# Projecting v, k and q of the first half of the tokens 512 columns at a time instead of 256

## The chip, the cores and the metric

The kernel runs on one core of one Trainium2 chip. The metric is the device time of one execution in microseconds (us); lower is better. The kernel before was timed in three runs: 2037.11, 2034.74 and 2035.24 us, median 2035.24 us. One further execution was profiled.

## The reference, cut to what matters

One layer of a streaming encoder is computed for 2048 prompt tokens and for 64 sample tokens of a running stream. All values are 32-bit floats.

```
h = rmsnorm(x, norm_g) @ w_in          # (tokens, 1024) @ (1024, 6144)
qa, ka, va, za, qb, kb, vb, zb, ga, gb = split(h)
qa, ka = rmsnorm per head of 64        # differential attention: q, k
k_prompt, v_prompt = ka, va            # outputs (also k_sample, v_sample)
oa = diff_attention(qa, ka, va)        # 4 heads, block-causal, ALiBi
ob = retention(qb, kb, vb)             # 4 heads, chunk by chunk
y  = x + (ga * (oa' @ w_oa) + gb * (ob' @ w_ob)) @ w_out
```

The change concerns the columns qa, ka and va (512 columns each) of the product with `w_in`, for prompt tokens 0 to 1023 and the 64 sample tokens.

## The kernel before, in words

**Products in three parts.** Every 32-bit operand of a large product is split into a high and a low part (`wh`, `wl` of the weights, `xh`, `xl` of the tokens) of a type that TensorE multiplies in one pass. A product is then three matmuls: high by high, high by low, low by high (`mm_group`, L375 to L390; the matmul is L384).

**Two halves.** The tokens are handled in two halves of 1024; the 64 sample tokens go with the first. For each half the normed tokens lie transposed in on-chip memory (`xh`, `xl`), and the 6144 columns of `w_in` are streamed past them. One pass over all tokens of a half with one block of columns is called a sweep here. There are 24 sweeps of 256 columns per half.

**Natural and transposed sweeps.** v, k, q and vb are computed by `natural` (L392): the tokens are the stationary operand (a tile of 128 tokens, or 64 for the sample tile), 256 columns of W are the moving one, and two token tiles share one PSUM bank (`mm`, two banks). The first half has nine token tiles, so a sweep has 9 x 24 matmuls. All other columns go through `transposed` (L548), where W is stationary and up to 512 tokens move.

**The supply of W.** A sweep needs four W units of 256 x 256. `w_load` (L332) brings each with one DMA of 256 KB into a staging buffer (`ws`, three of them). `w_split` (L344) casts it on ScalarE (`wh`, L354) and subtracts on GpSimd (`wl`, L361; the first and third on VectorE, L358); that frees the staging buffer. Units lie in the tag `w`: 12 buffers, a high and a low one to a unit, so six units. `mm_group` gives a unit back in the last token tile of the sweep (L388).

**Evacuation.** A finished bank is taken over by `fin_va` (L496: high part, plain copy, low part, three DMA stores) or `fin_qk` (L417: squares, gain, norm per head, transposes on TensorE at L466, high and low part of the transposed result, stores to `kT` or `qT` and for k to the output).

**The order of work.** The program plans itself: tasks are Python generators with priorities, `loop` (L80) emits the instructions of the most urgent task that is ready by the planner's own clock of the engines, and the order so found is fixed on TensorE, ScalarE and VectorE (L1546, L1564). The DMA queue on SyncE and the order on GpSimd are left to the framework. The projections (`w_stream`, L1442) have the lowest priority, attention (`z_stream`, L1497) goes ahead of them. Attention of half h starts when the mark `kqv0h` is set; heads 2 and 3 wait for `kqv1h` (L690). `ORD` (L1572) lists the sweeps of the two halves with these marks: in the first half v0, v1, k0, k1, q0, mark, q1, mark; in the second v0, k0, q0, mark, v1, k1, q1, mark. After that come vb, qb, kb, a mark for retention, and the gates. When all projections are stored, `out_stream` does the output projections.

**The start.** `x_prep` and `x_norm` (L247, L272) load and norm the token tiles, at most five in flight; `x_tile` (L298) transposes them on TensorE. The first sweep is told by `fresh` to wait for each token tile as it becomes ready.

**Buffers of the attention.** The pool `att` holds `K` (4 buffers), `V` (4) and `q` (2), each of 4 KB per partition; before the first attention they are empty. `load_head` (L649) and `load_q` (L674) fill them from the stores of the projections.

Of the kernel before, what the change touches and what calls it, by code (L numbers as in the profile page):

```python
# [54 lines left out]
class Hybrid:  # L55
# [105 lines left out]
    def consts(self):  # L161
# [11 lines left out]
        self.qinv = c("qinv", [128, 2, 8])  # L173
        for h in range(4):
            for u in range(2):
                nc.vector.memset(self.qinv[:, h // 2, 4 * u + 2 * (h % 2):4 * u + 2 * (h % 2) + 2],
                                 (SLOPES[h] / 0.125) ** 2 / 64.0)
        self.gq = c("gq", [128, 1])
# [153 lines left out]
    def w_load(self):  # L332
        for half in range(2):
            for c0 in self.order[half]:
                for q in range(4):
                    yield from self.take("ws")
                    st = self.sb(self.wp, [128, 2, 256], "ws")
                    t = self.ld(st, self.i["w_in"][0, 256 * q:256 * q + 256, c0:c0 + 256]
                                .rearrange("(c p) n -> p c n", p=128), 1 << 18)
                    self.wst.append((st, t))  # L340
                    self.wloads += 1
                    yield self.pe

    def w_split(self):  # L344
        nc = self.nc
        for n in range(4 * (len(self.order[0]) + len(self.order[1]))):
            yield lambda: len(self.wst) > 0
            st, t = self.wst.pop(0)
            yield from self.take("w", 2)
            if t > self.pe:  # L350
                yield t
            h = self.sb(self.wp, [128, 2, 256], "w", "wh", F32R)
            l = self.sb(self.wp, [128, 2, 256], "w", "wl", F32R)
            nc.scalar.copy(h, st)  # L354
            t = self.A(512, self.pe)
            if n in (0, 2):
                yield t
                nc.vector.tensor_sub(l, st, h.bitcast(F32))  # L358
                t = self.V(512, t)
            else:  # L360
                nc.gpsimd.tensor_sub(l, st, h.bitcast(F32))  # L361
                t = self.G(512, t)
            self.give("ws", t)
            self.wq.append((h, l, t))
# [10 lines left out]
    def mm_group(self, ps, n, us, wsl, x, wfirst, last):  # L375
        nc = self.nc
        seg, xsl = x
        for c in range(KC):
            a, b = yield from self.w_unit(us, c)
            a, b = a[:, wsl], b[:, wsl]  # L380
            xh, xl = self.xh[seg][:, c, xsl], self.xl[seg][:, c, xsl]
            ops = ((a, xh), (a, xl), (b, xh)) if wfirst else ((xh, a), (xh, b), (xl, a))
            for i, (p, q) in enumerate(ops):
                nc.tensor.matmul(ps, p, q, start=c == 0 and i == 0, stop=c == KC - 1 and i == 2)  # L384
                self.P(n)
            if c % 2:
                if last:
                    self.give("w", self.pe + LAT, 2)  # L388
                if c < KC - 1:
                    yield self.pe  # L390

    def natural(self, half, fin, fresh=False):  # L392
        us = []
        tiles = self.xtiles(half)
        for j0 in range(0, len(tiles), 2):
            pair = tiles[j0:j0 + 2]
            yield from self.take("mm")
            ps = self.psum("mm")
            for u, (src, r, seg, col) in enumerate(pair):
# [5 lines left out]
                if u < len(pair) - 1:  # L405
                    yield self.pe
            t0 = 1024 * half + 128 * j0 if j0 < 8 else T
            self.spawn(fin(ps[:r, :256 * len(pair)], r, len(pair), t0, self.pe + LAT), 0, "w")
            yield self.pe
# [7 lines left out]
    def fin_qk(self, which, g):  # L417
        nc = self.nc
        ep = self.ep

        def fin(ps, r, nu, t0, t):
            n, ng, rt = 256 * nu, 4 * nu, r * nu
# [21 lines left out]
            if which == "q":  # L444
                nc.vector.scalar_tensor_tensor(out=ms, in0=ms, scalar=64.0 * EPS,
                                               in1=self.qinv[:r, g, :ng], op0=ALU.add, op1=ALU.mult)
            else:
                nc.vector.tensor_scalar(ms, ms, 1.0 / 64, EPS, op0=ALU.mult, op1=ALU.add)
# [7 lines left out]
            if which == "k":  # L456
                if t0 < T:
                    dst = self.o["k_prompt"][0, 0, t0:t0 + rt, 2 * g:2 * g + 2]
                else:
                    dst = self.o["k_sample"][0, 0, :, 2 * g:2 * g + 2]  # L460
                ts = self.rows_out(dst.rearrange("t h c d -> t (h c d)"), raw, nu, 1 << 17)
            yield from self.take("tp")
            tp = self.psum("tp")
            for u in range(nu):
                for h in range(2):
                    nc.tensor.transpose(tp[:, h * rt + u * r:h * rt + u * r + r],  # L466
                                        raw[:, u * 256 + h * 128:u * 256 + h * 128 + 128],
# [5 lines left out]
            hi = self.sb(ep, [128, 512], "thi", dt=F32R)[:, :2 * rt]  # L473
            lo = self.sb(ep, [128, 512], "tlo", dt=F32R)[:, :2 * rt]
            pt = tp[:, :2 * rt]
# [12 lines left out]
            for d, s, tag, w in zip(dst, (hi, lo), ("thi", "tlo"), (t1, t2)):  # L488
                if w > self.pe:
                    yield w  # L490
                self.give(tag, self.st(d[2 * g:2 * g + 2, :, t0:t0 + rt].rearrange("h p t -> p h t"),
                                       s.bitcast(F32).rearrange("p (h t) -> p h t", h=2), nu << 17))
# [3 lines left out]
    def fin_va(self, g):  # L496
        nc = self.nc
        ep = self.ep

        def fin(ps, r, nu, t0, t):  # L500
            n, rt = 256 * nu, r * nu
# [13 lines left out]
            if t0 < T:  # L515
                dst = self.o["v_prompt"][0, 0, t0:t0 + rt, 2 * g:2 * g + 2]
            else:
                dst = self.o["v_sample"][0, 0, :, 2 * g:2 * g + 2]
            yield t1
            gsl = slice(256 * g, 256 * g + 256)  # L520
            self.give("thi", self.rows_out(self.vN[0][t0:t0 + rt, gsl], hi.bitcast(F32), nu, 1 << 17))
            yield t2
            td = self.rows_out(dst.rearrange("t h e -> t (h e)"), raw, nu, 1 << 17)
# [4 lines left out]
            self.give("tlo", self.rows_out(self.vN[1][t0:t0 + rt, gsl], lo.bitcast(F32), nu, 1 << 17))  # L528
# [913 lines left out]
    def w_stream(self):  # L1442
# [9 lines left out]
        first = ORD(fva0, fva, fk, fq, m0, m1)  # L1452
# [14 lines left out]
        self.order = [[c for c, _ in q if c is not None] for q in seqs]  # L1467
# [8 lines left out]
        for half in range(2):  # L1476
            for k, (c0, f) in enumerate(seqs[half]):
# [152 lines left out]
```

## Time and profile before

| what | before |
|---|---|
| timed runs, median | 2035.24 us |
| the profiled execution's own time | 2037.63 us |
| its span, first to last instruction | 2035.9 us |
| TensorE busy | 1999.1 us, 98% |
| TensorE weight loads busy | 1826.1 us, 90% |
| VectorE / ScalarE / GpSimd busy | 48% / 47% / 21% |
| DMA engines busy | 46.8% |
| granted TensorE clock, mean | 0.996 |

The span is a profiled execution's stretch from its first to its last instruction. The engines are PE (TensorE matmul), PEld (its weight loads, which overlap), DVE (VectorE), ACT (ScalarE), POOL (GpSimd) and SP (SyncE, which issues the DMAs). In a view by groups a row names the line, the engine, the operation, out<-in with shapes (partitions x elements; stationary operand first for a matmul), the count, the busy time and the mean of one in ns. In a timeline a row has the start in us, the duration in us and, in brackets, the idle time of the engine before it and what ended it. The duration of a matmul holds its whole way through the array, so that neighbours overlap: what a matmul costs in a stream is the distance from start to start. The view by windows gives, for each stretch, the busy time and the count of each engine, then the granted clock of TensorE, the share of DMA time and the bytes per second.

### The profile page before, as it was taken

The page shows a single profiled execution, that of the slowest core. Times are in us where ns is not written, and L with a number is a line of the kernel's source. Part 1 is how long each engine was busy: PE and PEld are TensorE (multiplying, and loading weights), DVE is VectorE, ACT ScalarE, POOL GpSimd, SP SyncE. Part 2 cuts the span into 40 slices and gives each one's busy share as a digit, 9 for nine tenths or more (in the row PEclk, how much of TensorE's full clock was granted, in tenths as well). Part 3 has the DMA queues.
Part 4 walks back from the last instruction along what each step waited for, and adds up shares of the span by engine and source line. Part 5 has one row for each costly group of instructions (what it writes and reads, how often), then busy time and mean ns, then how long its engine had stood idle before and what let it go on. Part 6 is the DMA issues. An engine that isn't in the chain of part 4 may idle for free. (4 is left out here: it accounts for less than half of the span.)

```text
span 2035.9 us, 35819 instructions
## 1 busy us (share of the span) xinstructions
PE 1999.1 (98%) x13058; PEld 1826.1 (90%) x13058; DVE 985.9 (48%) x2671; ACT 962.7 (47%) x2123; POOL 420.5 (21%) x394
## 2 busy tenths in 40 slices
PE   7999999999999999999999999999999979999999
PEld 7999999999998999999999888888888868888997
DVE  6265765643331210546856545635653365444442
ACT  5334766644343332535766655634654453333321
POOL 1222112121012221221211212122131343222210
PEclk9999999999999999999999999999999989999999
DMA  6663545345565463563352252463233665454531
GB/s 217 202 195 115 162 138 145 101 124 156 151 170 133 130 194 93 152 200 127 113 155 91 84 154 75 115 188 99 63 100 113 187 200 154 144 150 136 148 101 58
DMA packets 332160, 281.57 MB, mean 138 GB/s; under 512 B 65104, under 2 KB 307408, under 8 KB 331984
## 3 DMA queue, kind: packets, MB, share of 16 engines
q1 hardware_dynamic: 331984, 279.29, 46.8%
q8 instruction: 103, 1.69, 0.4%
q14 instruction: 73, 0.60, 0.1%
HBM read 187.71 MB, written 91.49 MB: 137 GB/s over the span
## 5 line engine op out<-in xcount | busy, mean ns | idle before, releaser
L384 PE MATMUL mm<-xh,wh 128*128 128x512 f32 (+2 forms) x1280 | 459.8, 359 | 0.0
L384 PE MATMUL mm<-xh,wl 128*128 128x512 f32 (+2 forms) x1280 | 452.0, 353 | 0.0
L384 PE MATMUL mm<-xl,wh 128*128 128x512 f32 (+2 forms) x1280 | 451.7, 353 | 0.0
L361 POOL TENSOR_TENSOR wl<-ws,wh 128x512 fp32r<-128x512 f32 x190 | 252.1, 1342 | 832.5 <-ACT wh L354 643.5
L384 PE MATMUL mm<-wh,xh 128*128 128x256 f32 x1088 | 313.3, 288 | 0.5 <-ACT xh L315 0.3
L384 PE MATMUL mm<-wl,xh 128*128 128x256 f32 x1088 | 307.7, 283 | 0.7 <-DVE wl L358 0.3
L384 PE MATMUL mm<-wh,xl 128*128 128x256 f32 x1088 | 307.7, 283 | 0.2 <-DVE xl L316 0.2
L384 PEld LDWEIGHTS mm<-xh,wl 128*128 128x128 f32 x1280 | 241.0, 188 | 31.1
L384 PEld LDWEIGHTS mm<-xh,wh 128*128 128x128 f32 x1280 | 241.3, 189 | 30.6 <-issue 0.2
L384 PEld LDWEIGHTS mm<-xl,wh 128*128 128x128 f32 x1280 | 241.4, 189 | 30.0
L384 PEld LDWEIGHTS mm<-wh,xh 128*128 128x128 f32 x1088 | 204.8, 188 | 3.3 <-ACT xh L315 0.5
L384 PEld LDWEIGHTS mm<-wl,xh 128*128 128x128 f32 x1088 | 204.9, 188 | 3.0 <-DVE wl L358 0.5
L384 PEld LDWEIGHTS mm<-wh,xl 128*128 128x128 f32 x1088 | 204.7, 188 | 0.4 <-DVE xl L316 0.4
L569 ACT COPY ev<-mm 128x512 f32<-128x512 f32 x140 | 71.6, 512 | 213.4 <-PE mm L384 200.4
L865 DVE TENSOR_TENSOR atl<-at,ath 128x512 fp32r<-128x512 f32 (+1 forms) x144 | 93.6, 660 | 151.6 <-ACT ath L863 151.6
L782 ACT ACTIVATE row<-row,a_mx 128x1024 f32<-128x1024 f32 (+7 forms) x160 | 153.5, 963 | 24.2 <-DVE a_mx L762 24.0
L752 DVE CUSTOM_DVE_ANT_0 row<-s,dfar 128x512 f32<-128x512 f32 (+2 forms) x192 | 117.3, 631 | 72.4 <-PE s L744 71.3
L354 ACT CAST wh<-ws 128x512 fp32r<-128x512 f32 x192 | 117.0, 619 | 65.4 <-PE mm L384 37.5
L863 ACT CAST ath<-at 128x512 fp32r<-128x512 f32 (+1 forms) x144 | 79.6, 563 | 99.1 <-PE at L850 98.6
L743 PE MATMUL s<-K,q 128*128 128x512 f32 (+3 forms) x320 | 120.3, 381 | 3.0 <-DVE a_acc L752 2.8
L803 DVE SCALAR_TENSOR_TENSOR row<-row,a_w 128x1024 f32<-128x1024 f32 (+4 forms) x96 | 101.4, 1064 | 40.5 <-ACT row L800 40.2
L744 PE MATMUL s<-K,q 128*128 128x512 f32 (+3 forms) x320 | 115.7, 363 | 0.0
(196 smaller groups left out, 3922.1 us busy)
## 6 DMA issues: line engine op xcount, KB each, us to landing
ws<-in_w_in_dram SPq DMA_DIRECT2D x192, 256.0 KB, 3.0
q<-qT SPq DMA_DIRECT2D x128, 128.0 KB, 3.0
V<-vN SPq DMA_DIRECT2D x24, 512.0 KB, 5.4
K<-kT SPq DMA_DIRECT2D x48, 256.0 KB, 4.2
gt<-gaT SPq DMA_DIRECT2D x64, 132.0 KB, 2.1
gt<-gbT SPq DMA_DIRECT2D x64, 132.0 KB, 2.1
xt<-in_x_prompt_dram SPq DMA_DIRECT2D x16, 512.0 KB, 5.0
kn<-in_cache_k_T_dram SPq DMA_DIRECT2D x32, 256.0 KB, 3.2
```

Source lines behind the costliest of these rows:

```text
L354: nc.scalar.copy(h, st)
L361: nc.gpsimd.tensor_sub(l, st, h.bitcast(F32))
L384: nc.tensor.matmul(ps, p, q, start=c == 0 and i == 0, stop=c == KC - 1 and i == 2)
L569: nc.scalar.copy(ev, ps)
L743: nc.tensor.matmul(ps, q1s, kk, start=True, stop=False)
L744: nc.tensor.matmul(ps, q2s, kk, start=False, stop=True)
L752: nc.vector.tensor_tensor_reduce(out=units[k0 // 1024][:, k0 % 1024:k0 % 1024 + n], in0=ps, in1=tab, scale=-SLOPES[h], scalar=3.0e38, op0= ...
L782: nc.scalar.activation(u, u, AF.Exp, bias=mx, scale=-1.0, accum_out=lp[:, k:k + 1])
L803: nc.vector.scalar_tensor_tensor(out=u0, in0=u0, scalar=w[:, 0:1], in1=u1, op0=ALU.mult, op1=ALU.add)
L863: nc.scalar.copy(ah[:, :w], at[:, :w])
L865: nc.vector.tensor_sub(al[:, :w], at[:, :w], ah[:, :w].bitcast(F32))
```

## The change

In the first half v, k and q are each computed in one sweep of 512 columns instead of two of 256. `natural` takes one token tile to a PSUM bank instead of two. `fin_qk` and `fin_va` take four heads of 128 tokens instead of two heads of 256 tokens, so the stores to `kT` and `qT` have rows of 128 tokens instead of 256, and those to `vN`, `k_prompt` and `v_prompt` rows of 512 columns instead of 256. A wide W unit is 256 x 512 and is brought by two DMAs through the same three staging buffers; it lies in one `K` and one `V` buffer, every fifth one in the two `q` buffers, so that five wide units fit. The first of its two subtractions is done on VectorE, the second on GpSimd. Both marks are set after the q sweep. The second half, and all other sweeps, are as before, in the tag `w`. A constant for q's norm gets eight more columns.

```diff
     def w_load(self):
         for half in range(2):
-            for c0 in self.order[half]:
+            for c0, wide in self.order[half]:
                 for q in range(4):
-                    yield from self.take("ws")
-                    st = self.sb(self.wp, [128, 2, 256], "ws")
-                    t = self.ld(st, self.i["w_in"][0, 256 * q:256 * q + 256, c0:c0 + 256]
-                                .rearrange("(c p) n -> p c n", p=128), 1 << 18)
...
+                    for j in range(1 + wide):
+                        yield from self.take("ws")
+                        st = self.sb(self.wp, [128, 2, 256], "ws")
+                        c = c0 + 256 * j
+                        t = self.ld(st, self.i["w_in"][0, 256 * q:256 * q + 256, c:c + 256]
+                                    .rearrange("(c p) n -> p c n", p=128), 1 << 18)
...
     def w_split(self):
...
+        for c0, wide in self.order[0] + self.order[1]:
+            for q in range(4):
+                if wide:
+                    tags = ("q", "q") if wides % 5 == 4 else ("K", "V")
+                    pool, width = self.ap, 512
+                    wides += 1
+                else:
+                    tags, pool, width = ("w", "w"), self.wp, 256
+                for j in range(1 + wide):
+                    yield lambda: len(self.wst) > 0
+                    st, t = self.wst.pop(0)
+                    if j == 0:
+                        for tag in tags:
+                            yield from self.take(tag)
+                        h, l = (self.sb(pool, [128, 2, width], tag, n, F32R) for tag, n in zip(tags, ("wh", "wl")))
+                    if t > self.pe:
+                        yield t
+                    hj, lj = h[:, :, 256 * j:256 * j + 256], l[:, :, 256 * j:256 * j + 256]
+                    nc.scalar.copy(hj, st)
+                    t = self.A(512, self.pe)
+                    if wide and j == 0:
+                        yield t
+                        nc.vector.tensor_sub(lj, st, hj.bitcast(F32))
+                        t = self.V(512, t)
+                    else:
+                        nc.gpsimd.tensor_sub(lj, st, hj.bitcast(F32))
+                        t = self.G(512, t)
+                    self.give("ws", t)
+                self.wq.append((h, l, t, tags))
...
                 if last:
-                    self.give("w", self.pe + LAT, 2)
+                    for tag in us[c // 2][3]:
+                        self.give(tag, self.pe + LAT)
...
-    def natural(self, half, fin, fresh=False):
+    def natural(self, half, fin, fresh=False, wide=False):
...
-        for j0 in range(0, len(tiles), 2):
-            pair = tiles[j0:j0 + 2]
+        per, n = (1, 512) if wide else (2, 256)
+        for j0 in range(0, len(tiles), per):
+            group = tiles[j0:j0 + per]
...
-                yield from self.mm_group(ps[:r, 256 * u:256 * u + 256], 256, us, slice(0, 256),
+                yield from self.mm_group(ps[:r, n * u:n * u + n], n, us, slice(0, n),
                                          (seg, slice(col, col + r)), False, j0 + u == len(tiles) - 1)
...
-        first = ORD(fva0, fva, fk, fq, m0, m1)
+        wva = (va, lambda half: self.natural(half, self.fin_va(0, 4), True, True), True)
+        wk = (ka, lambda half: self.natural(half, self.fin_qk("k", 0, 4), False, True), True)
+        wq = (qa, lambda half: self.natural(half, self.fin_qk("q", 0, 4), False, True), True)
+        first = ([wva, wk, wq, m0, m1], ORD(fva0, fva, fk, fq, m0, m1))
...
 def ORD(va0, va, k, q, m0, m1):
-    return ([va0, va[1], k[0], k[1], q[0], m0, q[1], m1],
-            [va0, k[0], q[0], m0, va[1], k[1], q[1], m1])
+    return [va0, k[0], q[0], m0, va[1], k[1], q[1], m1]
```

More of the change, by code (lines that the diff above doesn't have):

```diff
@@ L344, in w_split @@
     def w_split(self):
         nc = self.nc
[L346 to L364, printed above, removed]
+        wides = 0
@@ L527, in fin @@
             yield t3
-            self.give("tlo", self.rows_out(self.vN[1][t0:t0 + rt, gsl], lo.bitcast(F32), nu, 1 << 17))
+            self.give("tlo", self.rows_out(self.vN[1][t0:t0 + rt, gsl], lo.bitcast(F32), nu, nh << 16))
         return fin
@@ L1466, in w_stream @@
         seqs = [f + seq for f in first]
-        self.order = [[c for c, _ in q if c is not None] for q in seqs]
+        self.order = [[(c[0], len(c) > 2) for c in q if c[0] is not None] for q in seqs]
         self.seg_free = [0.0, 0.0]
@@ L1476, in w_stream @@
         for half in range(2):
-            for k, (c0, f) in enumerate(seqs[half]):
+            for k, (c0, f, *_) in enumerate(seqs[half]):
                 if c0 is None:
```

59 lines of the change are left out of this document (31 added, 28 removed).

## The prediction

> **What bounds the kernel now.** I read the engines' shares first, then the windows, then the waits of PE.
>
> ```profile
> span 2035.9 us, 35819 instructions
> PE 1999.1 (98%) x13058; PEld 1826.1 (90%) x13058; DVE 985.9 (48%) x2671; ACT 962.7 (47%) x2123; POOL 420.5 (21%) x394
> ```
> ```profile
> 0.00:10.00 10.00, 7.42 (x41) 6.99 (x41) 2.92 (x9) 4.77 (x9) 0.72 (x5) 1.00 0.81 262
> 10.00:25.00 15.00, 8.91 (x64) 7.76 (x64) 9.18 (x22) 13.05 (x32) 3.97 (x4) 0.94 0.88 308
> 25.00:40.00 15.00, 13.40 (x95) 12.97 (x96) 14.17 (x34) 8.46 (x20) 1.44 (x1) 0.83 0.45 119
> 60.00:100.00 40.00, 40.00 (x337) 40.00 (x337) 11.73 (x33) 11.12 (x24) 5.10 (x4) 1.00 0.71 222
> 1640.00:1690.00 50.00, 37.84 (x220) 33.92 (x221) 34.84 (x82) 31.00 (x83) 25.88 (x31) 0.90 0.68 207
> ```
> ```profile
> PE tp L308 <- DVE xl L316: 5.1, 1, 5.1
> ```
>
> PE is idle for 2035.9 - 1999.1 = 36.8 us in all: 2.6 us before 10 us, 6.1 + 1.6 = 7.7 us from 10 to 40 us (5.1 us of it one wait while token tiles arrive), 12.2 us where the output projections begin, the rest scattered. Elsewhere PE streams matmul after matmul, as from 60 to 100 us. So the path is PE's own program order. A change counts by what it does to the distance from one matmul to the next, and by the idle time that it makes or fills in the stage where nothing but projections can run: before attention begins.
>
> **The pace, and what the wide sweeps remove.** Two matmuls of 256 columns become one of 512. Their distances, from the timeline of PE: 256 columns with tokens stationary, 512 columns in a transposed sweep, 512 columns with the attention between, then the 64-token tile at 256 and a 64-token product at 512.
>
> ```profile
> 80.20 0.28 PE L384 MATMUL mm<-wh,xh 128*128 128x256 f32 x1
> ...
> 81.88 0.28 PE L384 MATMUL mm<-wh,xl 128*128 128x256 f32 x1
> ```
> ```profile
> 619.83 0.39 PE L384 MATMUL mm<-xl,wh 128*128 128x512 f32 x1
> ...
> 622.10 0.39 PE L384 MATMUL mm<-xh,wl 128*128 128x512 f32 x1
> ```
> ```profile
> 200.49 0.40 PE L744 MATMUL s<-K,q 128*128 128x512 f32 x1
> ...
> 201.19 0.28 PE L384 MATMUL mm<-wh,xh 128*128 128x256 f32 x1
> ```
> ```profile
> 51.70 0.28 PE L384 MATMUL mm<-wh,xh 128*64 128x256 f32 x1
> ...
> 54.32 0.28 PE L384 MATMUL mm<-wh,xl 128*64 128x256 f32 x1
> ```
> ```profile
> 2021.93 0.40 PE L1404 MATMUL at<-woh,ms 128*64 128x512 f32 x1
> ...
> 2023.79 0.39 PE L1406 MATMUL at<-woh,ms 128*64 128x512 f32 x1
> ```
>
> 80.20 to 81.88 are 14 steps: 120 ns. 619.83 to 622.10 are 10 steps: 227 ns. 200.49 to 201.19 are 3 steps: 233 ns. The sample tile: 23 steps, 114 ns; at 512 columns 8 steps, 233 ns. From 256 to 512 columns a matmul grows by 107 ns for 256 columns, so about 13 ns of each do not depend on its width; that is what a removed matmul gives back. In the first half six sweeps of 8 full tiles x 24 matmuls are 1152 matmuls; 576 go. 576 x (240 - 227) = 7.5 us saved; the sample tile's 144 matmuls become 72 and lose 72 x (233 - 228) = 0.3 us. **Term: -7.2 us.** The natural form at 512 columns does not occur in this trace: its bounds are the two 512-column rows, 227 and 233 ns; with 233 the term is 576 x 7 - 0.3 = -3.7 us. I take 227, the row of the same line with the same three-part alternation.
>
> On this the Trainium skill, "TensorE: Matmul & The Clock Gate", section "Wait — 56ns, not 53.3ns?", speaks against the change: it puts the fixed part of a warm matmul at about 2.5 ns. By that 648 removed matmuls would give 1.6 us, and the term would be -1.6 us. The 120 and 227 ns above agree with its slope and not with its fixed part.
>
> **The start.** A wide sweep's first tile needs all four wide units, which are eight loads, where the narrow one needed four. The casts, the loads through the queue on SP, and the cost of one load:
>
> ```profile
> 8.10 1.31 ACT L354 CAST wh<-ws 128x512 fp32r<-128x512 f32 x2 [1.53 <-DMA ws<-in_w_in_dram]
> ...
> 14.12 0.62 ACT L354 CAST wh<-ws 128x512 fp32r<-128x512 f32 x1 [1.76 <-DMA ws<-in_w_in_dram]
> ...
> 20.76 0.60 ACT L354 CAST wh<-ws 128x512 fp32r<-128x512 f32 x1
> ...
> 23.60 0.65 ACT L354 CAST wh<-ws 128x512 fp32r<-128x512 f32 x1
> ```
> ```profile
> 16.12 0.37 SPq L130 DMA_DIRECT2D ws<-in_w_in_dram  x1
> ...
> 22.77 0.41 SPq L130 DMA_DIRECT2D ws<-in_w_in_dram  x1
> ```
> ```profile
> L354 ACT CAST wh<-ws x192: 602/621/655, 8.1 to 1611.0; 128x512 fp32r<-128x512 f32 x192
> L361 POOL TENSOR_TENSOR wl<-ws,wh x190: 1261/1294/2114, 9.5 to 1611.9; 128x512 fp32r<-128x512 f32 x190
> L358 DVE TENSOR_TENSOR wl<-ws,wh x2: 693/693/693, 8.8 to 12.0; 128x512 fp32r<-128x512 f32 x2
> ...
> DMA to landing us min/median/max: 2.6/3.0/7.2
> ```
> ```profile
> 80.09 0.28 PE L384 MATMUL mm<-wh,xl 128*64 128x256 f32 x1
> ```
>
> The kernel before already issues eight loads by 22.77 us, so the DMA engines carry nothing more; the last four were only not needed yet. The eighth lands about 4 us after 22.77 (between median and longest), then cast 0.62 and subtraction 1.29: ready at 28.7 us. The last quarter of the first tile takes 6 x 0.227 = 1.4 us: 30.1. By then most token tiles are transposed, since PE does that while it waits. There follow 7 tiles x 24 x 0.227 = 38.1, the sample tile 24 x 0.233 = 5.6, and the transposes of the last two token tiles, about 1.8: the v sweep ends at 75.6 us. Before, both v sweeps end at 80.2 (the row at 80.09 is the last of the second). 2.4 us of the 4.6 are this sweep's share of the pace; 2.2 us remain, because the wait of 7.7 us between 10 and 40 us is in part replaced rather than added to. ACT works in order and its casts stand behind the norms of token tiles; if the eighth load takes 7.2 us and no more than three token tiles are transposed ahead, it is +5 us. **Term: -1 us, between -2 and +5**; I stay nearer to the computed end, since both loads' issue times are rows of this trace.
>
> The granted clock is 0.83 from 25 to 40 us. The same page's Part 1 says that an idle PE falls to half clock and is released after a busy window of about 3.4 us; an estimate by that is 1.7 us lost at 30 us, which would make the term about +1. Before pays such a stretch too, in the row of 0.83.
>
> **The two changes of sweep, v to k and k to q.** Before, six units fit: two of the next sweep lie ready, and three loads wait in staging. After, five wide units fit: one lies ready, and staging holds one and a half. Count from the start of the last (sample) tile, 1.4 us to a unit. Buffers come free at 1.4, 2.8, 4.2, 5.6; the next sweep's units are needed at 5.6, 7.0, 8.4, 9.8. Unit 2 is split from staging at once. The second half of unit 3 has to be loaded into the staging buffer that unit 2's first half frees at 1.4 + 0.2 + 0.62 + 0.69 = 2.9: landing 5.9 at best, with issue 6.3, cast 6.9, POOL 8.2; just in time. Unit 4's halves are issued at about 4.4 and land at 7.4 to 7.9, casts to 8.5, POOL to 9.9 against 9.8 needed. That is no slack, with ACT evacuating the last tiles in the same 5 us, and the SP queue putting stores between:
>
> ```profile
> 54.90 0.37 SPq L130 DMA_DIRECT2D ws<-in_w_in_dram  x1
> 55.36 0.48 SPq L130 DMA_DIRECT2D vN<-thi  x1
> 55.93 0.55 SPq L130 DMA_DIRECT2D out_v_sample_dram<-raw  x1
> 56.53 0.58 SPq L130 DMA_DIRECT2D vsN<-raw  x1
> 57.23 0.53 SPq L130 DMA_DIRECT2D vN<-tlo  x1
> 57.86 2.56 SPq L130 DMA_DIRECT2D ws<-in_w_in_dram  x3
> ```
>
> At the first change of sweep four stores put 3 us between a load and the next. No cover exists here: only projections run, and behind the waiting matmul stands all of PE. I take 1.5 us a change, half of that gap. **Term: +3 us, between 0 and +12** (the rival below gives the upper end). From q to vb there is none: the tag `w` is empty then, and six narrow units fit.
>
> **What I put at nothing.** The twelve subtractions that move to DVE, 12 x 0.69, hide in a DVE that is busy 11.73 of 40 us in that stage. Three small evacuations fewer are off PE. The stores to `kT` and `qT` get rows of 512 bytes; loads with such rows exist:
>
> ```profile
> V<-vN SPq DMA_DIRECT2D x24, 512.0 KB, 5.4
> ```
>
> Half as much is about 2.7 us; with the cast of 0.6 it stays below the 5.5 us of a tile, so the single `thi` buffer holds; without that cover each tile of k and q would wait on it. Attention begins one sweep later, about 20 us, and its loads can no longer go ahead of the q sweep:
>
> ```profile
> L743 PE MATMUL s<-K,q x320: 221/396/586, 194.3 to 1505.5; 128*128 128x512 f32 x88, 128*128 128x256 f32 x40, 128*128 128x384 f32 x24, 128*128 128x128 f32 x8
> busy tenths in 40 slices 0001222100000000002213212201210000000000
> ```
> ```profile
> L1133 PE MATMUL pv<-rvx,rqk x136: 269/275/320, 629.8 to 1576.4; 128*128 128x128 f32 x128, 64*64 64x128 f32 x8
> L384 PE MATMUL mm<-xh,wl x1280: 278/389/402, 277.8 to 1634.1; 128*128 128x512 f32 x110, 128*128 128x256 f32 x37, 128*128 128x320 f32 x36
> ```
>
> The second attention starts only in slice 18 (from 916 us), long after the first, and waits there for projections of the second half; retention ends at 1576.4 while projections run to 1634.1. So 20 us are absorbed twice, and PE fills the time with vb. If that cover were gone, up to 20 us would show.
>
> **Sum:** -7.2 - 1 + 3 = -5.2 us. The profiled execution has a span of 2035.9 us and took 2037.63, the rest lying around the span; by it the time would be 2032.4. It was 2.4 us above the median of the runs shown; from the median 2035.24 the forecast is **2030.0 us**.
>
> **The rivals.** About 0.2%, or 4 us, is what a measurement of this kernel can tell from no change.
> 1. Forecast, 2027 to 2031: chance 0.45.
> 2. Staging keeps up at both changes and the start gives its 2.2 us: -7.2 - 2.2 = -9.4, 2026, down to 2024: 0.10. For it: the chains above just fit.
> 3. The gain is eaten: pace at 233 ns (-3.7), start 0, changes +3: 2034.5, within 2031.2 to 2039.3: 0.22. For it: each wide chain has no slack.
> 4. The matmul's fixed part is a few ns when W moves over 512 columns: about -1.6 + 2 = 2035.6. Against it: 120 and 227 ns. 0.05. This is what the page's figure would do here.
> 5. Slower, W starved at the changes of sweep: the last two wide units come in two rounds through staging, each load 3.0 + cast 0.62 + POOL 1.29 + 1.5 in the SP queue = 6.4 us. From 2.9 us two rounds end at 15.7 against 9.8 needed: 5.9 us a change, 12 us for both, and one such round, 6 us, at the start: 12 + 6 - 7.2 = +11, 2046. It decides from 7.2 + 4 = 11 us of stalls together. For it: the gap of 3 us in the SP rows. 0.15.
> 6. The later attention comes onto the path: +20 - 5 = 2050. Against it: the last rows shown. 0.03.
>
> Faster by over 0.2% are 1 and 2: 0.55; within it 3 and 4: 0.27; slower 5 and 6: 0.18. The range leaves out the upper part of 5 and all of 6: 2024 to 2041; the likeliest case alone has 2027 to 2031.
>
> **What would show it.** Right: matmuls of 512 columns with `xh` stationary at 227 to 229 ns from start to start; the v sweep over at about 75 us; PE waits on `wl` or `wh` of 1 to 2 us at each of the two changes; first attention matmul near 210 us with the second starting no later than 916 us. Wrong: a distance of 233 ns or more, waits on `wl` of 5 us, or a first v sweep that ends past 80 us.

## The result, and the profile after

The changed kernel takes **2044.49 us** (median of six runs, 2041.63 to 2045.78) against 2035.49 us for the kernel before in the same comparison (six runs): a ratio of 1.0043, 95% interval 1.0030 to 1.0056. It is slower by 9 us, where 5 us of gain were forecast. Its profiled execution took 2044.45 us with a span of 2042.7 us, 6.8 us longer than the span before; the profiled execution before, with 2037.63 us, lies 2.1 us above the median of its kernel, and that is why the spans differ by 6.8 us and the medians by 9.0. From here on line numbers are those of the kernel of the quoted profile.

From the page of the changed kernel, the span and the first line of the engines:

```profile
span 2042.7 us, 34460 instructions
PE 2001.5 (98%) x12410; PEld 1794.4 (88%) x12410; DVE 990.3 (48%) x2669; ACT 958.7 (47%) x2112; POOL 409.8 (20%) x384
```

648 matmuls are gone (13058 to 12410), and yet PE is busy for 2.4 us more. Its view by windows, with the columns as before:

```profile
10.00:25.00 15.00, 7.50 (x28) 4.65 (x28) 9.75 (x23) 11.66 (x30) 2.23 (x2) 0.83 0.81 284
25.00:40.00 15.00, 11.43 (x42) 9.31 (x43) 14.23 (x30) 10.15 (x23) 4.73 (x3) 0.71 0.36 82
60.00:100.00 40.00, 36.23 (x145) 27.25 (x144) 11.31 (x26) 11.33 (x22) 5.97 (x4) 0.91 0.46 151
150.00:200.00 50.00, 49.23 (x218) 39.34 (x218) 26.61 (x56) 19.21 (x45) 9.65 (x8) 0.94 0.52 148
```

Three places are new. From 10 to 40 us PE is busy for 18.9 us, not 22.3, and the granted clock is 0.83 and 0.71 (before 0.94 and 0.83): by these shares 13.8 us at half clock, where before had 6.9. From 60 to 100 us, where before PE never paused, 3.8 us are idle and the clock is 0.91. From 150 to 200 us it is 0.94. The waits of PE up to 220 us name what it waited for:

```profile
PE mm L398 <- ACT wh L368: 5.7, 3, 2.5
PE tp L309 <- DVE x_st L285: 4.8, 1, 4.8
PE mm L398 <- POOL wl L375: 3.2, 5, 0.9
PE tp L309 <- DVE xl L317: 2.9, 2, 2.2
```

Casts and subtractions of W units make up 8.9 us in eight waits.

**An account of where PE falls behind.** For the comparisons I use one derived number. Each matmul of a trace is given a standard distance by its moving width: 227.3 ns at 512 columns, 173.5 at 384, 146.7 at 320, 122.0 at 264, 119.4 at 256, 109.5 below (the medians of the distances in the trace of before are 227, 176, 147, 122 and 120 ns, and 109 at 128 columns). The time since the span's start, less the sum for the matmuls started by then, is called the **lag**; at the end it is taken when the last matmul starts, 4.5 us before the span's end in these two. It holds waits and slow clock together, and a kernel with fewer or wider matmuls gets no credit in it. In us:

| kernel | lag at 40 | 60 | 100 | 160 | 280 | end | sum of distances | time, ratio |
|---|---|---|---|---|---|---|---|---|
| before | 17.0 | 17.2 | 17.3 | 19.1 | 21.5 | 70.7 | 1960.7 | 2035.49 |
| after | 23.5 | 23.6 | 31.1 | 37.6 | 38.6 | 84.9 | 1953.3 | 2044.49, 1.0043 |

The sum of distances falls by 7.4 us, 648 x (2 x 119.4 - 227.3) ns. That is the pace by the standard distances and not a measurement of its own; by the 229 ns of the next rows and the prediction's 120 ns it is 576 x (240 - 229) = 6.3 us on the full token tiles. The lag rises by 14.2: +6.4 in the start, +7.4 more at the change from v to k (by 100 us), +4.7 by 160 us (the kernel before loses 1.8 there), -1.4 by 280, -2.9 behind it. 14.2 - 7.4 = 6.8 us, the difference of the spans. Each row of the lags is one profiled execution, and executions of one kernel differ by some us (the profiled ones lie between 2.7 us below and 2.2 us above their kernel's median), so differences of 2 to 3 us behind 280 us carry little.

**The pace.** PE in the changed kernel's v sweep, timeline:

```profile
63.77 0.39 PE L398 MATMUL mm<-wh,xh 128*128 128x512 f32 x1
...
66.97 0.39 PE L398 MATMUL mm<-wh,xl 128*128 128x512 f32 x1
```

14 steps in 3.20 us: 229 ns, the distance that the prediction named.

**The change from v to k.** First PE, then the queue of SP, then POOL and ACT:

```profile
88.12 0.51 PE L398 MATMUL mm<-wl,xh 128*128 128x512 f32 x1 [0.63 <-POOL wl L375]
...
92.09 0.79 PE L398 MATMUL mm<-wh,xh 128*128 128x512 f32 x1 [2.53 <-ACT wh L368]
93.50 0.79 PE L398 MATMUL mm<-wl,xh 128*128 128x512 f32 x1 [0.61 <-POOL wl L375]
94.09 0.63 PE L398 MATMUL mm<-wh,xl 128*128 128x512 f32 x1
94.52 0.63 PE L398 MATMUL mm<-wh,xh 128*128 128x512 f32 x1
...
97.93 0.63 PE L398 MATMUL mm<-wh,xl 128*128 128x512 f32 x1
```
```profile
81.87 1.61 SPq L130 DMA_DIRECT2D ws<-in_w_in_dram  x2
85.16 0.48 SPq L130 DMA_DIRECT2D vN<-thi  x1
...
88.10 7.43 SPq L130 DMA_DIRECT2D ws<-in_w_in_dram  x6
```
```profile
86.27 1.80 POOL L375 TENSOR_TENSOR wl<-ws,wh 128x512 fp32r<-128x512 f32 x1 [3.20 <-ACT wh L368]
85.51 1.27 ACT L368 CAST wh<-ws 128x512 fp32r<-128x512 f32 x2
91.42 1.99 ACT L368 CAST wh<-ws 128x512 fp32r<-128x512 f32 x3 [4.64 <-DMA ws<-in_w_in_dram]
```

Read it from the bottom. ACT casts two halves at 85.51 and then has nothing for 4.64 us, because the next load was issued only at 88.10: right after POOL's subtraction from 86.27, which frees a staging buffer, had ended at 88.07, and 0.54 us after the last of the four stores of v that start at 85.16. PE waits 0.63 + 2.53 + 0.61 = 3.8 us for casts and subtractions of W. Then something follows that no wait shows: from 94.09 to 97.93 the matmuls come 427 ns apart, at half clock. The clock is half for 6.8 us, from 91.6 us on; half of that, 3.4 us, is an estimate of what it costs. 3.8 + 3.4 = 7.2 of the 7.4 us.

**The change from k to q**, PE of the same kernel:

```profile
147.61 0.63 PE L484 MATMUL tp<-ident,raw 128*128 128x128 f32 x4 [0.55 <-DVE raw L469]
...
149.43 0.64 PE L398 MATMUL mm<-wh,xh 128*128 128x512 f32 x1 [1.19 <-ACT wh L368]
...
150.84 0.80 PE L398 MATMUL mm<-wl,xh 128*128 128x512 f32 x1 [0.77 <-POOL wl L375]
```

Waits of 2.5 us, and again 6.8 us at half clock, from 149.6 us: by the same estimate 2.5 + 3.4 = 5.9 us, of 6.2 us that the lag grows from 144 to 160 us.

### The profile page after: what moved, and what is told of

The parts are those of the page before. It is cut to its first block, busy times and chain, and to the rows that moved or that the text cites. A ratio compares the mean times of both kernels' runs of the same rounds, so it can differ in the third digit from the quotient of the medians.

```text
span 2042.7 us, 34460 instructions
## 1 busy us (share of the span) xinstructions
PE 2001.5 (98%) x12410; PEld 1794.4 (88%) x12410; DVE 990.3 (48%) x2669; ACT 958.7 (47%) x2112; POOL 409.8 (20%) x384
## 5 line engine op out<-in xcount | busy, mean ns | idle before, releaser
L375 POOL TENSOR_TENSOR wl<-ws,wh 128x512 fp32r<-128x512 f32 x180 | 242.5, 1359 | 842.2 <-ACT wh L368 518.7
L398 PE MATMUL mm<-wh,xh 128*128 128x256 f32 (+3 forms) x872 | 278.4, 319 | 7.2 <-ACT wh L368 5.7
L398 PE MATMUL mm<-wl,xh 128*128 128x256 f32 (+3 forms) x872 | 273.5, 314 | 3.2 <-POOL wl L375 3.2
L398 PE MATMUL mm<-wh,xl 128*128 128x256 f32 (+3 forms) x872 | 272.7, 313 | 0.0
L398 PEld LDWEIGHTS mm<-xl,wh 128*128 128x128 f32 x1280 | 241.5, 189 | 29.3
L398 PEld LDWEIGHTS mm<-wh,xh 128*128 128x128 f32 (+1 forms) x872 | 165.6, 190 | 20.1 <-ACT wh L368 6.8
L398 PEld LDWEIGHTS mm<-wl,xh 128*128 128x128 f32 (+1 forms) x872 | 165.6, 190 | 16.4 <-POOL wl L375 5.3
L398 PEld LDWEIGHTS mm<-wh,xl 128*128 128x128 f32 (+1 forms) x872 | 165.6, 190 | 10.7
```

Source lines behind the costliest of these rows:

```text
L375: nc.gpsimd.tensor_sub(lj, st, hj.bitcast(F32))
```

## The experiments

Twelve kernels ran, each timed in five rounds against the kernel before. The explanation that I held first: the loss lies in the staging of W, at the start and at the two changes of sweep, each wait being paid a second time in clock. That the two engines that subtract and the order of the loads at the start have a part in it came in with e5 and e10. Its rivals: the attention that begins later, a pace that is not there. Each expectation says what it takes up. All lags:

| kernel | lag at 40 | 60 | 100 | 160 | 280 | end | sum of distances | time, ratio [95%] |
|---|---|---|---|---|---|---|---|---|
| e1 | 19.1 | 20.9 | 23.2 | 30.4 | 32.0 | 79.7 | 1953.3 | 2041.71, 1.0024 [1.0015, 1.0034] |
| e2 | 21.3 | 21.5 | 21.6 | 28.8 | 29.6 | 77.9 | 1955.8 | 2041.85, 1.0022 [1.0014, 1.0031] |
| e3 | 23.5 | 24.1 | 24.3 | 26.2 | 28.6 | 75.9 | 1958.3 | 2042.86, 1.0028 [1.0018, 1.0039] |
| e4 | 16.6 | 16.9 | 16.8 | 18.8 | 20.6 | 70.4 | 1960.7 | 2037.43, 1.0000 [0.9991, 1.0009] |
| e5 | 16.2 | 20.0 | 20.7 | 24.9 | 25.9 | 76.7 | 1953.3 | 2034.14, 0.9987 [0.9978, 0.9996] |
| e6 | 16.7 | 16.9 | 18.7 | 23.8 | 24.9 | 76.4 | 1955.8 | 2038.57, 1.0010 [1.0001, 1.0018] |
| e7 | 23.3 | 23.6 | 29.3 | 36.0 | 37.3 | 86.9 | 1953.3 | 2047.39, 1.0048 [1.0035, 1.0061] |
| e8 | 23.3 | 23.4 | 25.0 | 28.5 | 29.7 | 78.8 | 1959.0 | 2043.47, 1.0029 [1.0018, 1.0040] |
| e9 | 15.1 | 19.3 | 20.0 | 22.6 | 23.8 | 72.5 | 1953.3 | 2032.33, 0.9979 [0.9970, 0.9988] |
| e10 | 10.6 | 18.8 | 20.5 | 23.1 | 24.1 | 73.1 | 1953.3 | 2032.29, 0.9977 [0.9967, 0.9987] |
| e11 | 22.2 | 22.5 | 22.6 | 24.5 | 27.1 | 75.2 | 1960.7 | 2042.11, 1.0023 [1.0015, 1.0032] |
| e12 | 10.8 | 10.9 | 11.6 | 14.5 | 15.7 | 64.7 | 1953.3 | 2026.16, 0.9947 [0.9933, 0.9960] |

The kernel before took 2036.45 to 2036.90 us in these comparisons. It took 2035.49 us in the comparison with the changed kernel, so times from different comparisons are compared by their distance from the kernel before. For e8 the sum of distances holds the added matmuls.

**e1: staging without a shortage.** The wide loads go to the tag `w` (12 buffers, empty in that stage) instead of `ws` (3).

```diff
-                        yield from self.take("ws")
+                        tag = "w" if wide else "ws"
+                        yield from self.take(tag)
...
-                    self.give("ws", t)
+                    self.give("w" if wide else "ws", t)
```

> The changed kernel, but the 256-column loads of wide units are staged in the twelve empty buffers of tag w instead of the three of ws. Theory 1 (W starved by staging at the start and at the two changes of sweep, and the clock that falls to half behind each wait): the waits of 3.8 us and 2.0 us at the changes and their two stretches at half clock (3.4 us each) go, so 2044.5 - 10 = 2034 to 2036 us, granted clock 1.0 from 60 to 200 us. Rival 2 (attention that starts 38 us later comes onto the path): no change, 2043 to 2046. Rival 3 (512 columns in the natural form give no pace): 2036 to 2038.

Measured: 2041.71 us, where 2034 to 2036 were expected. The change from v to k shrinks from 7.4 to 2.0 us (lag from 21.2 at 84 us to 23.2 at 100), as expected: that wait was staging. The change from k to q does not shrink (7.2 us from 100 to 160 us, 6.5 in the changed kernel), and its cause is another one. DVE, POOL and PE at that place:

```profile
137.58 0.67 DVE L373 TENSOR_TENSOR wl<-ws,wh 128x512 fp32r<-128x512 f32 x1
138.18 1.25 DVE L227 SCALAR_TENSOR_TENSOR sm_t<-sm_y 128x8 f32<-128x8 f32 x1
139.47 1.22 DVE L228 TENSOR_TENSOR sm_t<-sm_t,ms 128x8 f32<-128x8 f32 x1
140.72 1.19 DVE L229 SCALAR_TENSOR_TENSOR sm_y<-sm_t,sm_y 128x8 f32<-128x8 f32 x1
141.94 1.71 DVE L470 TENSOR_TENSOR raw<-raw,sm_y 128x512 f32<-128x512 f32 x1
```
```profile
137.58 7.20 POOL L376 TENSOR_TENSOR wl<-ws,wh 128x512 fp32r<-128x512 f32 x5 [2.95 <-ACT wh L369]
```
```profile
143.80 1.09 PE L485 MATMUL tp<-ident,raw 128*128 128x128 f32 x4 [2.90 <-DVE raw L470]
```

While POOL subtracts five halves in a row, each of the three small DVE operations (eight columns, steps of the norm of k) lasts 1.2 us. The k tile's `raw` is late by that, and PE's transposes, next in its fixed order, wait 2.90 us. With more staging POOL works in a longer run, and DVE stands still for longer.

**e2 and e3: one part alone.** e2 keeps v narrow, e3 has v alone wide:

```diff
-        first = ([wva, wk, wq, m0, m1], ORD(fva0, fva, fk, fq, m0, m1))
+        first = ([fva0, fva[1], wk, wq, m0, m1], ORD(fva0, fva, fk, fq, m0, m1))
```
```diff
-        first = ([wva, wk, wq, m0, m1], ORD(fva0, fva, fk, fq, m0, m1))
+        first = ([wva, fk[0], fk[1], fq[0], m0, fq[1], m1], ORD(fva0, fva, fk, fq, m0, m1))
```

> The changed kernel with v back in two narrow sweeps; k and q stay wide, both marks after q. Theory 1: the start is that of before, the units for k are split ahead into empty buffers, and only the change from k to q starves: 2035.5 - 4.8 (pace of k and q) + 5.4 (2.0 us wait and 3.4 us of half clock) = 2036 us. Rival 2: attention is as late as in the change, so 2041 to 2044.

> Only v is wide; k and q are narrow as before, with the mark after q's first sweep. Theory 1: the start alone, 4.0 us lost up to the end of the v sweep: 2039.5 us. Rival 2: attention hardly later than before, 2035 to 2036.

Measured: 2041.85 and 2042.86 us, where 2036 and 2039.5 were expected. e2 lies in the range of its rival, the later attention; e4 speaks against that. e3 loses its time in the start (lag 24.1 at 60 us, +6.9 against before) and nowhere else up to 160 us. e2 loses 7.2 us at the change from k to q. But it had 4.3 us too many at 60 us, with a narrow v sweep as before. That was not expected, and it led to e11: in the change a narrow unit's subtraction always goes to POOL, also the first and the third, which the kernel before gave to DVE.

**e11: two subtractions.** The kernel before, with these two on POOL:

```diff
-            if n in (0, 2):
+            if n < 0:
```

> The kernel before, with the first and third subtraction of W on GpSimd like all others, nothing else. The run with v narrow had this, and its first sweep ended 4.5 us later. Theory: the start hangs on these two operations, 2036.5 + 4 = 2040 us. Rival (that start came from another order of loads): 2036 to 2037.

Measured: 2042.11 us; lag 22.5 instead of 17.2 at 60 us. Two operations of 0.69 us on another engine cost 5.3 us. PE's longest wait there:

```profile
30.53 1.12 PE L308 MATMUL tp<-ident,xt 128*128 128x128 f32 x4 [7.53 <-DVE xl L316]
```

It was 5.09 us, ending at 25.96. The start is thus as sensitive to who subtracts as to when W comes.

**e4: the later attention by itself.** The kernel before, with both marks set after q1.

```diff
-    return ([va0, va[1], k[0], k[1], q[0], m0, q[1], m1],
+    return ([va0, va[1], k[0], k[1], q[0], q[1], m0, m1],
```

> The kernel before, all sweeps narrow, with both marks of the first half set after the second q sweep, so that attention starts about 28 us later. Theory 1: 2034.5 to 2036.5 us, no change. Rival 2: 2040 us or more.

Measured: 2037.43 us, ratio 1.0000. The first row of the scores, after the edit:

```profile
L743 PE MATMUL s<-K,q x320: 221/396/628, 221.8 to 1504.7; 128*128 128x512 f32 x88, 128*128 128x256 f32 x40, 128*128 128x384 f32 x24, 128*128 128x128 f32 x8
```

Attention begins at 221.8 us instead of 194.3 and ends where it ended (1505.5 before). Nothing of these 27.5 us reaches the path, to within 1.8 us by the interval. In the changed kernel it begins 11 us later still; that part is not tested by itself.

**e5 and e7: both wide subtractions on DVE**, with wide staging (e5, on e1) and with the three buffers of the change (e7).

```diff
-                    if wide and j == 0:
+                    if wide:
```

> The run that stages wide loads in w, with both subtractions of a wide unit on VectorE, none on GpSimd. In that run the small VectorE operations of k's norm took 1.2 us beside GpSimd's subtractions against 0.17 us elsewhere, and PE waited 2.9 us for the transposes behind them. Theory 1b (VectorE is held by GpSimd, and the wait costs a stretch at half clock too): the q sweep shortens from 60.4 to about 53 us, and the v sweep by 1 to 3 us: 2041.7 - 7 to - 10 = 2032 to 2035 us. Rival (the wait is W, not the norm): 2040 to 2043, q sweep 60 us.

> The changed kernel with both subtractions of a wide unit on VectorE; staging stays at three buffers. If the waits at the changes of sweep come from loads that have no staging buffer: they stay, 2042 to 2045 us. If they come from VectorE and GpSimd holding each other: 2036 to 2039.

Measured: 2034.14 us, as expected, and 2047.39 us, which is 2.4 us above the range of the first case. Subtracting on DVE is worth nothing without the wide staging: e7 keeps the wait for W at both changes (lag 23.6, 29.3, 36.0 at 60, 100, 160 us, as the changed kernel), e5 loses 0.7 us at the first change and 4.2 by 160 us. In e5 the holding-up has moved on: the subtractions of vb's narrow units, still on POOL, run from 138.76 us (three in 4.89 us), three of DVE's four small operations on k's last tile take 1.07, 1.23 and 1.23 us beside them, the fourth, at 143.71 us behind POOL's run, 0.16, and PE waits 2.59 us for a `wl` of DVE.

**e9: vb's first eight units on DVE too.**

```diff
-                    if wide:
+                    if wide or late < 8:
+                        late += not wide
```

> The run with staging in w and wide subtractions on VectorE, and also the eight narrow subtractions for the vb sweeps on VectorE. There GpSimd's three subtractions for vb ran in the middle of the change from k to q, VectorE's small operations took 1.07 to 1.23 us beside them, and PE waited 2.6 us. Theory 1b: that wait goes, 2034.1 - 3 = 2031 us, ratio 0.997 to 0.998. Rival (VectorE is simply full there): 2034 or more.

Measured: 2032.33 us, ratio 0.9979: faster than before, and as expected. The last three of these four operations, without POOL beside them:

```profile
140.21 0.15 DVE L227 SCALAR_TENSOR_TENSOR sm_t<-sm_y 64x8 f32<-64x8 f32 x1
140.40 0.16 DVE L228 TENSOR_TENSOR sm_t<-sm_t,ms 64x8 f32<-64x8 f32 x1
140.59 0.16 DVE L229 SCALAR_TENSOR_TENSOR sm_y<-sm_t,sm_y 64x8 f32<-64x8 f32 x1
```

0.15 to 0.16 us each, at the same place of the work. From 60 to 160 us it loses 3.3 us, where the changed kernel loses 14.0 and the kernel before 1.9.

**e6: k and q wide, v and its start as before**, with the wide units staged in `w` and subtracted on DVE.

```diff
+                        if wide:
+                            yield lambda: self.nsplit >= 8
...
+                    if wide or self.nsplit in (1, 3):
```

> v narrow with the first and third subtraction on VectorE as in the kernel before; k and q wide, their loads staged in w once v is split, their subtractions on VectorE. Theory 1 with 1b: the start of before (v done at 80.4 us) and two wide sweeps of 53 us in place of 56: 2036.4 - 5.5 = 2031 us, ratio 0.997. Rival (512 columns give no pace on this path): 2036.

Measured: 2038.57 us, a miss of 7.6 us. The start is that of before (lag 16.9 at 60 us). Its pace gives 4.9 us, but 3.4 us of lag come by 280 us (vb's units are on POOL in it) and another 2.3 behind it. I did not follow the latter.

**e8: fill the pauses of PE**, to price the clock. Needless matmuls of 512 columns, whose results nobody uses, are put ahead of the late units of the changed kernel:

```diff
+            if fill and c in fill:
+                hold = self.psum("at")
+                for _ in range(fill[c]):
+                    nc.tensor.matmul(hold, self.xh[0][:, 0, 0:128], self.xh[0][:, 0, 0:512], start=True, stop=True)
...
+        wk = (ka, lambda half: self.natural(half, self.fin_qk("k", 0, 4), False, True, {2: 3, 4: 10, 6: 3}), True)
+        wq = (qa, lambda half: self.natural(half, self.fin_qk("q", 0, 4), False, True, {4: 6, 6: 3}), True)
```

> The changed kernel with 16 needless matmuls of 512 columns (3.6 us) ahead of the waiting units in k's first tile and 9 (2.0 us) in q's, results unused. Theory (of the 7 to 8 us lost at the two changes, 3.4 us each are a clock that falls to half after the wait): the clock stays at 1.0 from 60 to 200 us, PE work fills the idle time, 2044.5 - 5 to - 7 = 2038 to 2040 us. Rival (the clock does not matter, only the wait): 2044 to 2047.

Measured: 2043.47 us. By windows:

```profile
60.00:100.00 40.00, 39.09 (x171) 30.29 (x170) 9.74 (x26) 11.35 (x22) 6.29 (x4) 1.00 0.45 151
150.00:200.00 50.00, 49.32 (x232) 39.39 (x233) 23.60 (x54) 19.26 (x45) 7.65 (x6) 1.00 0.55 154
```

The clock stays at 1.00 in both stretches, and the q sweep ends at 200.5 us instead of 203.9. So 5.7 us of extra matmuls came for less than nothing: half clock after the pauses was real time. Of the 3.4 us about 2 are left at the end (7.0 us above the kernel before in its comparison, the changed kernel 9.0), where 5 to 7 were expected, and the two intervals overlap. The account shows the rest lost behind 280 us: from there to the end the lag grows by 49.1 us in e8, 49.2 in before, but only 46.3 in the changed kernel. Over all kernels that number runs from 46.3 to 51.5. Why the changed kernel's is the smallest stays open; single executions of one kernel differ by as much (e8's runs by 4.2 us).

**e10: W ahead of the token tiles.** e9, with the loads of x held back until W's are issued:

```diff
-            yield lambda: self.xfly < XFLY and (half > 0 or self.wloads >= min(2 * j, 4))
+            yield lambda: self.xfly < XFLY and (half > 0 or self.wloads >= min(4 * j, 8))
```

> The run before this one, and the third and later token tiles are loaded only after eight loads of W. Theory (the first wide tile waits for its eight loads, casts and subtractions, which stand behind the norms of five token tiles): the start up to 60 us loses 3 us less, 2028 us. Rival (the token tiles then come late instead): 2031 or more.

Measured: 2032.29 us, no better than e9, where 2028 was expected; the rival's time came, but not by late token tiles. By 40 us the start had gained 4.5 us (lag 10.6), and by 60 us it was gone again (18.8). ACT, then the SP queue in front of it:

```profile
51.88 0.59 ACT L528 CAST thi<-mm 128x512 fp32r<-128x512 f32 x1 [8.66 <-DMA vN<-thi]
```
```profile
40.24 1.50 SPq L130 DMA_DIRECT2D ws<-in_w_in_dram  x3
41.77 0.54 SPq L130 DMA_DIRECT2D dfar<-in_c_dfar_dram  x1
44.56 0.34 SPq L130 DMA_DIRECT2D dnear<-in_c_dnear_dram  x1
44.94 0.44 SPq L130 DMA_DIRECT2D state<-in_state_ret_dram  x1
45.89 0.33 SPq L130 DMA_DIRECT2D vN<-thi  x1
```

The cast of the next tile's high part waits 8.66 us for the store of the last one. That store was issued at 45.89, 4.5 us after the part had been cast, behind W loads and three first loads of other stages, and it landed 6 us later. There is one `thi` buffer.

**e12: two buffers for the high part of v.** e10, with the wide v sweep's high part in `ath` (two buffers of the attention, empty then):

```diff
+        ht = "ath" if nh == 4 else "thi"
...
-            yield from self.take("thi")
+            yield from self.take(ht)
```

> As the run with W's loads ahead of the token tiles, but the high part of v in the wide sweep alternates between two buffers (the attention's still empty ath) instead of the one thi buffer. In that run 8.2 us were lost between 40 and 60 us, 8.66 us of them beside a cast of thi that waited for the store of the tile before it. Theory 1 (the single buffer is what holds it): no wait of over 2 us on that cast, the lag at 60 us falls from 18.8 to 11 to 14 us, the v sweep ends at 73 to 76 us, and the time falls by 4 to 7 us to 2026 to 2028.5. Rival 2 (the DMA queue on SP is late for all three stores of a tile, and the next buffer takes the wait over): the wait moves to the plain copy or to the low part, the lag at 60 us stays over 17 us, the time 2031 to 2033.5. Rival 3 (the start gains, but it is given back behind 200 us, as 2 of the 3 us that the filled pauses won were): lag at 60 us 11 to 14 us, yet the time over 2029.5.

Measured: **2026.16 us, ratio 0.9947 [0.9933, 0.9960]**, the fastest of all, inside the range of theory 1. Its windows:

```profile
10.00:25.00 15.00, 11.30 (x52) 8.21 (x53) 12.20 (x28) 13.55 (x32) 0.00 (x0) 1.00 1.06 377
25.00:40.00 15.00, 15.00 (x80) 12.59 (x79) 14.12 (x32) 10.75 (x25) 0.00 (x0) 1.00 0.95 289
40.00:60.00 20.00, 20.00 (x102) 16.26 (x101) 8.26 (x27) 6.43 (x14) 0.00 (x0) 1.00 0.71 255
```

PE is busy throughout from 25 us, the clock never falls below 1.00 up to 280 us, and the v sweep ends at 71.8 us (84.5 in the changed kernel, 80.4 before). The lag is 10.9 at 60 us and 64.7 at the end: what the start won was kept to the end. Whether the kernel before would gain from the same two edits to its start was not tried, so how much of this time is owed to the wide sweeps is not shown.

## Why the prediction was wrong

- **The pace** (-7.2 us) was right to within 1 us: 229 ns from start to start against the 227 taken, which makes it 6.3 us. The 233 ns of rival 3 did not come, nor did the few ns of rival 4: 240 - 229 = 11 ns went with each removed matmul.
- **The start** (-1, between -2 and +5) was the first wrong term: +6.4 us by 60 us. The step that failed is "the kernel before already issues eight loads by 22.77 us ... the last four were only not needed yet". Three staging buffers had to carry eight halves: timeline rows of the changed kernel, SP and then ACT:

```profile
12.85 3.26 SPq L130 DMA_DIRECT2D ws<-in_w_in_dram  x3
...
27.37 0.93 SPq L130 DMA_DIRECT2D ws<-in_w_in_dram  x2
```
```profile
24.87 1.12 ACT L368 CAST wh<-ws 128x512 fp32r<-128x512 f32 x2
...
30.97 0.60 ACT L368 CAST wh<-ws 128x512 fp32r<-128x512 f32 x1
```

  The eighth load went out at 27.37, not 22.77, because the casts that free staging stand behind the norms of the token tiles in ACT's order (the sixth and seventh are in the row at 24.87); POOL's subtraction behind them ended at 27.34, and the load followed at once. Its cast began at 30.97, where the sum implied 26.8, and the v sweep ended at 84.5 us, past the 80 that the prediction had named as a sign against it. Of the 6.4 us, 3.4 are more idle time of PE from 10 to 40 us; the rest goes with 6.9 us more at half clock, which the prediction had seen and left out of the sum. The runs split the term: more staging takes the lag at 40 us from 23.5 to 19.1 (e1), subtracting on DVE to 16.2 (e5), vb's on DVE too to 15.1 (e9), loading W ahead of the tokens to 10.6 (e10). A term that a store's buffer adds between 40 and 60 us (8 us in e10, 0.1 in e12) was not in my sum at all: I had tested the one `thi` buffer against the steady rhythm of k and q (the stores to `kT` and `qT` land 2.3 to 2.5 us after issue there, below the 2.7 that I took), not against a queue full of first loads.
- **The two changes of sweep** (+3, between 0 and +12) were the second: 7.4 and 6.2 us in the changed kernel where it loses them, 12.1 net of what the kernel before loses by 160 us, the upper end of the range. The chain that the prediction worked out, "no slack" with stores in the queue, is the one in the rows at 81.87 to 91.42, and e1 shows that staging was its cause at the first change. At the second, staging alone did not help (e1), and staging with the subtractions on DVE did (e5, e9). I took half of one gap in the queue as the price. The wait was 3.8 us, and it was nearly doubled by the clock, which I had weighed at the start only.
- **What I put at nothing**: the twelve subtractions "hide in a DVE that is busy 11.73 of 40 us". Shares of busy time were the wrong evidence. e1, e5, e9 and e11 show that it matters which of DVE and POOL subtracts and what the other does at that moment: DVE's subtraction is 0.69 us and short, POOL's 1.3 us and holds DVE up. Leaving the other twelve of the 24 wide subtractions on POOL was the mistake, once staging is wide; with three staging buffers moving them too gained nothing (e7). That narrow units lost their two subtractions on DVE is in the diff, and in the changed kernel no narrow unit comes in the start; it hit e2 only.
- **The later attention** was rightly put at nothing, as far as e4 tests it, though it began at 232.7 us and not near 210.
- **The rivals**: the outcome is rival 5 (2046 forecast, chance 0.15). Its places were right: W starved at the start and at both changes. That its size came so near was in part luck: it priced a wait of 5.9 us for two rounds through staging at each change, and the waits were 3.8 and 2.5 us, with about 3.4 us of slow clock behind each, which it did not hold; at the second change its mechanism is only part of the cause. I gave it a small chance since the chain "just fits"; the rows of before had shown the four stores in the queue.

## What to carry to other kernels

Here removing instructions from the bound engine paid only once what feeds it had slack at the places where it starts anew: count for each such place the staging buffers, the queue's order and the engine that frees the buffer, at that moment and not in shares. Doubling the width of one operand doubles the first delivery, and here the staging had to widen with it. And when a change loses, look for its gain before undoing it: here the pace was there all along, and three edits to the supply (e9) with two to the start (e10, e12) turned +9 us into -10.7.

## What the runs showed of the hardware

- **A short wait is paid twice.** At the two changes PE waited for 3.8 us within 6.0 us and for 2.5 us within 3.8 us, and at each the clock was half for 6.8 us, an estimated 3.4 us more. A single wait of 2.59 us (e5) brought none, one of 2.90 us (e7) a stretch of 3.4 us. What decides is in the clock records of the traces. In each trace all stretches at half clock begin on one grid with steps of 3.41 us. Over the fourteen traces, each step at full clock in which PE was idle for 1.94 us or more was followed by half clock (66 of 66), and none in which it was idle for less than 1 us (0 of 8046); between the two, 12 of 98 were. The 2.59 us of e5 fall into two steps, 1.21 and 1.38 us; of the 2.90 us of e7, 2.89 fall into one. The Trainium skill, "TensorE: Matmul & The Clock Gate", Part 1, has a window of about 3.4 us that runs freely. That agrees with the grid; that half clock comes only after a whole idle window, as it says, does not agree with the second change, where the clock fell at 149.65 us after 0.55 + 1.19 = 1.74 us of waits.
- **POOL stops DVE, but not in all that it does.** In the kernel before too, DVE and then POOL:

```profile
108.18 0.42 DVE L435 TENSOR_TENSOR raw<-mm,gk 64x256 f32<-64x256 f32 x1 [0.79 <-ACT sq L429]
108.52 0.15 DVE L226 SCALAR_TENSOR_TENSOR sm_t<-sm_y 128x8 f32<-128x8 f32 x1
108.70 1.20 DVE L227 TENSOR_TENSOR sm_t<-sm_t,ms 128x8 f32<-128x8 f32 x1
109.94 0.17 DVE L228 SCALAR_TENSOR_TENSOR sm_y<-sm_t,sm_y 128x8 f32<-128x8 f32 x1
```
```profile
106.07 3.81 POOL L361 TENSOR_TENSOR wl<-ws,wh 128x512 fp32r<-128x512 f32 x3 [20.32 <-PE mm L384]
```

  Within POOL's run from 106.07 to 109.88 the operation that reads PSUM keeps its 0.42 us; the one on 128 x 8 elements with both inputs in SBUF takes 1.20, until POOL is done. (The 0.15 us ahead of it fall where POOL goes from its second subtraction to its third, at about 108.6 us.) The Trainium skill, "SBUF — State Buffer", section "Who interferes with whom", says that the two engines share one pair of ports, as a lock, and that an operation of DVE with two inputs in SBUF meets POOL's reads. These rows agree. An operation with one input in SBUF can be held too: the `TENSOR_SCALAR` on the same 128 x 8 elements takes 0.17 us in the median of e1 and 1.27 at 133.39 us, beside POOL.
- **Two operations of 0.69 us moved the end by 5.3 us** (e11), in a stage where every engine waits for another in a fixed order.
